# A fourth chunk of x turned by VectorE blocks in a hybrid attention and LRU layer

## The chip, the cores and the metric

The kernel runs on one core of one Trainium2 chip. Its time is the device time of one execution in microseconds; the table below gives the median of three runs of the kernel before. The profile is of one further execution. TensorE (PE in the profile) multiplies matrices, VectorE (DVE), ScalarE (ACT) and GpSimd (POOL) work elementwise, and SyncE (SP) issues most of the transfers between DRAM and the on-chip memory (SBUF).

## What is computed

One layer of an encoder for 512 tokens of width 2048, all in float32. Only the beginning matters here: an RMS norm and one projection, whose columns are then divided among attention heads, a linear recurrence and their gates.

```python
def hybrid_layer(x, norm_w, w_in, ...):
    h = rms_norm(x, norm_w)                       # x * rsqrt(mean(x*x) + eps) * norm_w
    proj = jnp.einsum('bsd,de->bse', h, w_in)     # (512, 2048) x (2048, 4608)
    q, k, v, g_attn, xr, g_lru = jnp.split(proj, SPLITS, axis=-1)
    attn_out = attention_group(q, k, v, q_norm_w, k_norm_w)
    lru_out = lru_group(xr, conv_w, conv_b, ...)
    mixed = jnp.concatenate([rms_norm(attn_out, attn_norm_w) * jax.nn.silu(g_attn),
                             rms_norm(lru_out, lru_norm_w) * jax.nn.silu(g_lru)], axis=-1)
    return x + jnp.einsum('bse,ed->bsd', mixed, w_out)
```

## The kernel before

Each float32 matrix is kept as two parts, a high one in the faster float32r format and a low one with what is left; a product is three matmuls (`mm3`: high by high, high by low, low by high). The rows of x enter the products without their norm: the factor per token, from the sum of the squares of its row, is multiplied in when the first sums are taken out of PSUM (`rbc`, line 471). So the squares are needed only when the first four sums are complete.

The first projection is `proj_feat(C_XR, a1, ...)`. It computes 512 columns of the recurrence's input in four PSUM banks and goes over the 2048 inner features in eight chunks (c = 0 to 7) of 256, two tiles of 128 each (kk = 2c and 2c + 1). A chunk needs the weights of its 256 features and x of these features *with the features along the partitions*. In DRAM x has the tokens along the rows, so it has to be turned. A chunk is 24 matmuls: four blocks of columns (e = 0 to 3) with six each, and after each block the generator yields the step (c, e).

`xchunk(c)` brings chunk c of x in several steps, taken one by one with `next`. Below, "x4" is the chunk c = 4 of x, "w4" the weights of chunk 4, and "s4" the splitting of these weights in high and low parts (`wsplit`, lines 218 and 219). There are two ways to turn:

- On TensorE (`xturn`), for c below `TURNED` = 5: load; eight transposes of 128 x 128 into PSUM (line 253); ScalarE takes the high part out with the norm's weight (258), VectorE the low part (261); VectorE squares the loaded chunk and sums along the row (272).
- By blocks, for c from 5 on: load; VectorE transposes blocks of 32 x 32 (`blocks`, 281), which leaves blocks in the wrong quarter of the partitions; `put_aside` writes them to DRAM with one transfer (289), `bring_back` reads them in the right order with four (296); ScalarE scales by the norm's weight (338) and casts the high part, VectorE subtracts for the low part (both 339). ScalarE squares the loaded chunk (268).

The order of instructions has three sources. TensorE's is that of the program. SP's is that of the program up to `s1.close()` (line 1234), and ScalarE's and VectorE's up to `s2.close()` (step (1, 2)). Everything else is placed by a planner, by readiness and by priority: `tc.high_priority(AHEAD)` raises the priority of what stands in its block by 600 places, and `tc.issue_after(i)`, or `behind(those)` for several, keeps what is in its block behind i on i's engine, without waiting for i's end. All engines execute their own queues in order; SP, too, waits with a transfer until its data and its buffer are there, and with it everything behind.

What happens at which step of the projection is written out in the table `moves` (line 1195): the entry (2, 0) "x5 x4 x5" takes one step of chunk 5, one of chunk 4 and one more of chunk 5 after the first block of chunk 2. A w loads weights, an s splits them. Loads of weights go through a ring with three places (`wring`), the split parts through four places each (`wh`, `wl`: two chunks).

The statistics (`xstats`, line 371) run in two steps, at (4, 3) and at (7, 0). The first adds up the eight chunks' squares on VectorE (373), takes the inverse root on GpSimd (346, 347) and lays the result out on VectorE (357 to 360). The second spreads it over the partitions with two matmuls on TensorE (367) and copies it (368). These two matmuls stand in TensorE's order behind step (7, 0).

Of the kernel before, what the change touches and what calls it, by code (L numbers as in the profile page):

```python
# [20 lines left out]
KT = DM // P  # L21
# [15 lines left out]
AHEAD = 600  # L37
# [12 lines left out]


B = 32
TURNED = 5
NQ = P // B


# [7 lines left out]
def hybrid_kernel(  # L64
# [20 lines left out]
    nc = tc.nc  # L85
# [32 lines left out]
    def nm(s):  # L118
        cnt[0] += 1
        return f"{s}_{cnt[0]}"  # L120

    def x2():
        return pools["xw"].tile([P, SEQ], F32R, tag="x2", bufs=32, name=nm("x2"))
# [19 lines left out]
    def mm():  # L143
        return ps.tile([P, SEQ], F32, tag="mm", name=nm("mm"))

    def const(shape, name, dt=F32):
        return cp.tile(list(shape), dt, tag=name, name=name)

    def f(ap):
        return ap.bitcast(F32)  # L150
# [58 lines left out]
    turn_of, split_done = [0], {}  # L209
# [19 lines left out]

    xh, xl = [None] * KT, [None] * KT  # L230
    ssq = const([P, NT, KT // 2], "ssq")
    highs, x_parts, squared = {}, [], []

    def xload(c, nk=1):

        xc = b4(shape=(P, NT, 2 * P))
        for k in range(nk):
            ks = slice(k * 2 * P // nk, (k + 1) * 2 * P // nk)
            cs = slice(c * 2 * P + ks.start, c * 2 * P + ks.stop)
            nc.sync.dma_start(xc[:, :, ks], xf[:, cs].rearrange("(t p) d -> p t d", p=P))  # L240
            yield xc

    def behind(those):
        stack = ExitStack()
        for ins in those:
            stack.enter_context(tc.issue_after(ins))
        return stack

    def xturn(xc, kk, then=None):
        pt = mm()  # L250
        for t in range(NT):
            ks = slice(kk % 2 * P, (kk % 2 + 1) * P)
            nc.tensor.transpose(pt[:, t * P : (t + 1) * P], xc[:, t, ks], ident)  # L253
        if then:
            then()
        xh[kk], xl[kk] = x2(), x2()
        with behind(split_done[-1] if kk > 3 else ()):
            highs[kk // 2] = nc.scalar.activation(
                xh[kk], pt, AF.Identity, scale=nw[:, kk : kk + 1]
            ).ins  # L260
        nc.vector.scalar_tensor_tensor(
            xl[kk], pt, nw[:, kk : kk + 1], f(xh[kk]), op0=ALU.mult, op1=ALU.subtract
        )

    def xsquare(xc, c):
        for t in range(NT):
            if c >= TURNED:
                nc.scalar.activation(
                    xc[:, t, :], xc[:, t, :], AF.Square, accum_out=ssq[:, t, c : c + 1]
                )  # L270
                continue
            square = nc.vector.scalar_tensor_tensor(
                xc[:, t, :], xc[:, t, :], 1.0, xc[:, t, :], op0=ALU.mult, op1=ALU.mult,
                accum_out=ssq[:, t, c : c + 1],
            )
            if c == 1:
                squared.append(square.ins)

    def blocks(u, t, src):

        nc.vector.transpose(
            u[:, :, :, t, :].rearrange("p b k r -> p k b r"),
            src.rearrange("p (k b c) -> p k b c", k=2, c=B),
        )

    def put_aside(u, tag, bufs):

        aside_ = dram.tile([P, NQ, 2 * SEQ // NQ], F32, name=nm(tag), tag=tag, bufs=bufs)
        nc.sync.dma_start(aside_, u.rearrange("p b k t r -> p b (k t r)"))
        return aside_  # L290

    def bring_back(to, aside_):

        src = aside_.rearrange("(i c) b x -> b c i x", c=B)
        for b in range(NQ):
            nc.sync.dma_start(
                to[b * B : (b + 1) * B].rearrange("p i k t r -> p i (k t r)"), src[b]
            )

    def in_order(v):  # L300
        return v.rearrange("p (t i r) -> p i t r", t=NT, i=NQ)

    def xchunk(c):
        with tc.high_priority(AHEAD):
            (xc,) = xload(c)
        yield
        if c < TURNED:
            with tc.high_priority(AHEAD):
                for k in range(2):
                    xturn(xc, 2 * c + k)  # L310
            if c == 2:
                yield
            with behind(split_done[2][1:] if c == 2 else ()):
                xsquare(xc, c)
            yield
            return
        u, back = (
            ring.tile([P, NQ, 2, NT, B], F32, name=nm("xu")) for ring in (aring, hring)
        )
        with tc.high_priority(AHEAD), tc.issue_after(squared[-1] if c == TURNED else split_done[3][1]):  # L320
            for t in range(NT):
                blocks(u, t, xc[:, t, :])
        yield
        with tc.high_priority(AHEAD):
            there = put_aside(u, "xd", KT // 2 - TURNED)
        with tc.issue_after(highs[TURNED - 1]):
            xsquare(xc, c)
        yield
        with tc.high_priority(AHEAD):
            bring_back(back, there)  # L330
        yield
        with tc.high_priority(AHEAD), behind(split_done[-1]):
            for k in range(2):
                kk = 2 * c + k
                xh[kk], xl[kk] = x2(), x2()
                hi, lo = (in_order(v) for v in (xh[kk], xl[kk]))
                v = back[:, :, k]
                nc.scalar.activation(v, v, AF.Identity, scale=nw[:, kk : kk + 1])
                x_parts[:] = nc.scalar.copy(hi, v).ins, nc.vector.tensor_sub(lo, v, f(hi)).ins
        yield  # L340

    last_pool = [None]
# [288 lines left out]
    def sent(es, nh, *us):  # L631

        us = us or [
            pools["rot"].tile([P, NQ, 2, NT, B], F32, tag="uq", bufs=2, name=nm("uq"))
            for _ in range(nh // 2)
        ]
        for n, u in enumerate(us):
            for t, e in enumerate(es):
                blocks(u, t, e[:, 2 * n : 2 * n + 2].rearrange("p h d -> p (h d)"))
            yield  # L640
            asides.append(put_aside(u, "qd", 5))
# [7 lines left out]
    def split_head(pair, k, hi, lo):  # L649
        src = pair[:, :, k]  # L650
        hi, lo = (in_order(v) for v in (hi, lo))
        return nc.scalar.copy(hi, src).ins, nc.vector.tensor_sub(lo, src, f(hi)).ins
# [509 lines left out]
    s2 = ExitStack()  # L1162
# [4 lines left out]
    with tc.high_priority():  # L1167
        xs, ws = xload(0, 2), wraw(w_in, 0, C_XR, 2)
        nc.scalar.dma_start(nw_st, norm_w.rearrange("(k p) -> k p", p=P))
        xc, raw = next(xs), next(ws)  # L1170
        next(xs), next(ws)
        table = const([P, 1], "table")
        nc.scalar.activation(table, ones[:, :1], AF.Exp)
        first = []

        def scales():
            columns(nw, nw_st)
            first.append(wsplit(raw, 0, nc.vector.tensor_copy))

        xturn(xc, 0, scales)  # L1180
        busy(WARM2)
    stats = xstats()
    chunks = [xchunk(c) for c in range(1, KT // 2)]

    raws = {}
# [5 lines left out]
    def split_x(c):  # L1191
# [1 line left out]
            given[c] = [wsplit(raws[c], k) for k in range(2)]  # L1193

    moves = {
# [6 lines left out]
    }  # L1202

# [8 lines left out]
    for step in proj_feat(C_XR, a1, first, given):  # L1212
        if step is None:
            with tc.high_priority():
                first.append(wsplit(raw, 1))
                xturn(xc, 1)
            xsquare(xc, 0)
            move(None)
            given[1] = wload(w_in, 2 * P, C_XR)
            continue  # L1220
        c, e = step
        move(step)
        if (c, e) == (1, 2):
            s2.close()
        if (c, e) == (4, 2):
            with tc.high_priority(AHEAD):
                vec_load()
        if (c, e) == (7, 1):
            columns(vec, vec_st)
        if (c, e) in ((4, 3), (KT // 2 - 1, 0)):  # L1230
            with tc.high_priority(AHEAD), tc.issue_after(split_done[-1][1]):
                next(stats)
# [216 lines left out]
```

## Time and profile before

| | |
|---|---|
| median of three runs | 627.94 us (627.38 to 628.29) |
| profiled execution | 627.43 us |
| its span, first to last instruction | 625.6 us |
| mean granted clock of TensorE | 0.999 |
| TensorE busy | 620.6 us, 99% of the span |
| VectorE, ScalarE, GpSimd busy | 79%, 56%, 16% |
| bytes moved by DMA | 127.61 MB, 204 GB/s on the mean |

A row of the timeline has the start and the duration in microseconds, the engine, the line, the operation, what it writes and reads, the shapes and how many instructions are merged into the row; in brackets stand the idle time of the engine ahead of it and what ended that. `SPq` is SP's queue: a row there is the issue of a transfer, not the transfer. Rows of groups give the busy time, the mean duration in nanoseconds of one instruction, and the idle time ahead. Names such as `b` (loaded x), `xu` (blocks of x, both before and after their way), `xd` (their copy in DRAM), `x` (high and low parts of x), `wr` (loaded weights) and `wh`, `wl` (their parts) are tiles.

### The profile page before, as it was taken

The numbers are of one execution on the slowest core, as the hardware profiler recorded it, in microseconds if no ns is written. First come the engines' busy times: TensorE is split into PE (matmuls) and PEld (weight loads), VectorE is DVE, ScalarE is ACT, GpSimd is POOL, SyncE is SP. The second block draws the span as 40 slices with busy tenths as digits, with TensorE's granted clock in tenths as the row PEclk, the third lists the DMA queues.
The fourth block names the chain that finished last, engine by engine and source line by source line (L and its number), as shares of the span: only waits on it lengthen the run. The fifth ranks groups of instructions, "written<-read, shape, count | busy, mean of one in ns | idle before, by whom it ended". The sixth has DMA issues, their size and how long they took to land.

```text
span 625.6 us, 8287 instructions
## 1 busy us (share of the span) xinstructions
PE 620.6 (99%) x2761; PEld 513.1 (82%) x2761; DVE 494.3 (79%) x795; ACT 353.1 (56%) x618; POOL 101.6 (16%) x134
## 2 busy tenths in 40 slices
PE   9999999999999999999999999999999999999997
PEld 7888888888888888888888888888888888888886
DVE  5967979986699876887887888549978866887886
ACT  3764899479946823545485548328445633443441
POOL 0000211112003621522123223100210101010010
PEclk9999999999999999999999999999999999999999
DMA  8987785759774599479669646923995777897262
GB/s 290 308 224 218 179 199 172 176 135 198 236 234 136 170 246 241 98 204 268 193 173 260 201 137 194 259 85 104 273 245 180 212 250 244 290 320 237 69 202 101
DMA packets 73595, 127.61 MB, mean 204 GB/s; under 512 B 6617, under 2 KB 29265, under 8 KB 73553
## 3 DMA queue, kind: packets, MB, share of 16 engines
q1 hardware_dynamic: 65664, 109.65, 56.5%
q0 software_dynamic: 7712, 17.31, 14.3%
q8 instruction: 21, 0.34, 0.2%
q14 instruction: 22, 0.17, 0.1%
q10 hardware_dynamic: 176, 0.14, 0.1%
HBM read 110.29 MB, written 37.75 MB: 237 GB/s over the span
## 4 chain that ended last, share of the span: by engine, by line
PE 99%; DVE 0%; issue 0%; POOL 0%; POOLq 0%
PE pj L153 21%; PE pj L155 21%; PE pj L154 21%; PE mm L1029 14%; PE pj L1029 11%; PE mm L155 3%; PE mm L153 3%; PE mm L154 3%; PE pj L388 1%; PE mm L253 1%; PE mm L1156 1%; PE mm L829 0%; PE mm L367 0%; DVE cb L1058 0%; PE mm L189 0%
## 5 line engine op out<-in xcount | busy, mean ns | idle before, releaser
L153 PE MATMUL pj<-x,wh 128*128 128x512 f32 x376 | 146.7, 390 | 0.0
L155 PE MATMUL pj<-x,wl 128*128 128x512 f32 x376 | 146.3, 389 | 0.0
L154 PE MATMUL pj<-x,wh 128*128 128x512 f32 x376 | 146.3, 389 | 0.0
L218 ACT CAST wh<-wr 128x512 fp32r<-128x512 f32 x143 | 85.1, 618 | 81.8 <-PE pj L154 32.0
L219 DVE TENSOR_TENSOR wl<-wr,wh 128x512 fp32r<-128x512 f32 x144 | 99.6, 720 | 21.3 <-ACT wh L218 20.2
L881 ACT CAST wh<-wr 128x1024 fp32r<-128x1024 f32 (+1 forms) x72 | 60.7, 860 | 74.8 <-PE mm L1029 35.4
L882 DVE TENSOR_TENSOR wl<-wr,wh 128x1024 fp32r<-128x1024 f32 (+1 forms) x72 | 68.7, 984 | 29.9 <-ACT wh L881 29.8
L155 PEld LDWEIGHTS pj<-x,wl 128*128 128x128 f32 x376 | 70.6, 188 | 14.8
L154 PEld LDWEIGHTS pj<-x,wh 128*128 128x128 f32 x376 | 70.6, 188 | 14.6
L153 PEld LDWEIGHTS pj<-x,wh 128*128 128x128 f32 x376 | 70.6, 188 | 14.5
L153 PE MATMUL pj<-wh,x 128*128 128x512 f32 x192 | 74.7, 389 | 0.0
L155 PE MATMUL pj<-wh,x 128*128 128x512 f32 x192 | 74.7, 389 | 0.0
L154 PE MATMUL pj<-wl,x 128*128 128x512 f32 x192 | 74.7, 389 | 0.0
L905 POOL DMA_DIRECT2D t<-in_w_out_dram x40 | 33.6, 897 | 157.1 <-DMA t<-in_w_out_dram 99.4
L1029 PE MATMUL mm<-wh,ml 128*128 128x512 f32 x126 | 49.0, 389 | 0.0
L1029 PE MATMUL mm<-wh,mh 128*128 128x512 f32 x126 | 49.0, 389 | 0.0
L1029 PE MATMUL mm<-wl,mh 128*128 128x512 f32 x126 | 49.0, 389 | 0.0
L154 PEld LDWEIGHTS pj<-wl,x 128*128 128x128 f32 x192 | 36.0, 188 | 7.6
L155 PEld LDWEIGHTS pj<-wh,x 128*128 128x128 f32 x192 | 36.0, 188 | 7.5
L153 PEld LDWEIGHTS pj<-wh,x 128*128 128x128 f32 x192 | 36.0, 188 | 7.4
L706 POOL TENSOR_SCALAR p<-p,sm 128x512 f32<-128x512 f32 x32 | 24.2, 762 | 88.7 <-DVE sm L705 88.7
L1029 PE MATMUL pj<-wl,mh 128*128 128x512 f32 (+1 forms) x100 | 38.5, 385 | 0.0
(201 smaller groups left out, 1041.0 us busy)
## 6 DMA issues: line engine op xcount, KB each, us to landing
wr<-in_w_in_dram SPq DMA_DIRECT2D x71, 512.0 KB, 4.8
wr<-in_w_out_dram SPq DMA_DIRECT2D x24, 512.0 KB, 5.1
t<-in_w_out_dram POOLq DMA_DIRECT2D x40, 256.0 KB, 7.0
wr<-t SPq DMA_DIRECT2D x40, 256.0 KB, 5.8
pd<-u SPq DMA_DIRECT2D x16, 512.0 KB, 3.0
pt<-pd SPq DMA_DIRECT2D x64, 128.0 KB, 4.0
t<-in_w_out_dram SPq DMA_DIRECT2D x24, 256.0 KB, 5.6
t<-t SPq DMA_DIRECT2D x16, 256.0 KB, 5.5
```

Source lines behind the costliest of these rows:

```text
L153: nc.tensor.matmul(acc, lh, rh, start=start, stop=False)
L154: nc.tensor.matmul(acc, lh, rl, start=False, stop=False)
L155: nc.tensor.matmul(acc, ll, rh, start=False, stop=stop)
L218: copy(hi, raw[:, k, :]).ins,
L219: nc.vector.tensor_sub(lo, raw[:, k, :], f(hi)).ins,
L253: nc.tensor.transpose(pt[:, t * P : (t + 1) * P], xc[:, t, ks], ident)
L388: nc.tensor.matmul(acc[e], w[:, e * P : (e + 1) * P], x_[k], start=k == 0 and j == 0, stop=False,)
L706: last_pool[0] = nc.gpsimd.tensor_scalar(p, p, sm, 0.0, op0=ALU.mult, op1=ALU.add).ins
L881: nc.scalar.copy(hi[:, to], b)
L882: nc.vector.tensor_sub(lo[:, to], b, f(hi[:, to]))
L905: nc.gpsimd.dma_start(dst, src, accum_op=ALU.add)
L1029: nc.tensor.matmul(dst[s][:, es], lh[:, ts_], rh[:, es], start=i == ends_[0] and j == 0, stop=i == ends_[1] and j == 2,)
```

## The change

`TURNED` becomes 4, so chunk 4 is turned by VectorE's blocks too: TensorE has eight transposes less. Its blocks do not go through DRAM. A new function, `carry`, moves them from SBUF to SBUF in twelve pieces of 32 partitions (32 KB each): nine issued by SP, three by GpSimd, and the four blocks that stay in their quarter are copied by GpSimd. Chunks 5 to 7 go through DRAM as before, `put_aside` and `bring_back` now with a step between them.

The squares of chunk 4 go from VectorE to ScalarE, behind the last high part that is taken out of PSUM. The squares of chunks 5 and 6 are put behind ScalarE's cast of chunk 5's high part, those of chunk 7 behind that of chunk 6. The block transposes of chunks 5 to 7 and the finishing of chunk 4 have new places to stand behind. The table of steps is written anew: the loads go out in the order x2 x4 w2 x3 x5 w3 x6 w4 x7 (before: x2 x3 w2 x5 x4 w3 x6 x7 w4), then the carry of x4, then x5's write, w5, x6's write, x5's way back, w6, x7's write, x6's and x7's way back, w7.

```diff
-TURNED = 5
+TURNED = 4
...
     def xsquare(xc, c):
...
-            square = nc.vector.scalar_tensor_tensor(
+            nc.vector.scalar_tensor_tensor(
...
+    def carry(to, u):
+
+        def at_(v, b):
+            return v[b * B : (b + 1) * B]
+
+        for d in range(1, NQ):
+            for b in range(NQ):
+                i = (b + d) % NQ
+                queue = nc.gpsimd if b == NQ - 1 else nc.sync
+                queue.dma_start(at_(to, b)[:, i], at_(u, i)[:, b])
+        for b in range(NQ):
+            nc.gpsimd.tensor_copy(at_(to, b)[:, b], at_(u, b)[:, b])
+
...
+    raw_x, blocked = {}, {}
+
+    def lows_of(c):
+        return {4: (), 5: (lows.get(2),), 6: split_done.get(3), 7: split_done.get(3)}[c][-1:]
 
     def xchunk(c):
...
-        with tc.high_priority(AHEAD), tc.issue_after(squared[-1] if c == TURNED else split_done[3][1]):
+        raw_x[c] = xc
+        with tc.high_priority(AHEAD), behind(lows_of(c)):
             for t in range(NT):
-                blocks(u, t, xc[:, t, :])
+                blocked[c] = blocks(u, t, xc[:, t, :])
         yield
         with tc.high_priority(AHEAD):
-            there = put_aside(u, "xd", KT // 2 - TURNED)
-        with tc.issue_after(highs[TURNED - 1]):
-            xsquare(xc, c)
-        yield
-        with tc.high_priority(AHEAD):
-            bring_back(back, there)
-        yield
-        with tc.high_priority(AHEAD), behind(split_done[-1]):
+            if c == TURNED:
+                carry(back, u)
+            else:
+                there = put_aside(u, "xd", KT // 2 - TURNED - 1)
+                yield
+                bring_back(back, there)
+        if c == TURNED:
+            with tc.issue_after(highs[c - 1]):
+                xsquare(xc, c)
+        yield
+        with tc.high_priority(AHEAD), behind(
+            (*split_done[-1], blocked[TURNED + 1]) if c == TURNED else split_done[-1]
+        ):
             for k in range(2):
...
                 nc.scalar.activation(v, v, AF.Identity, scale=nw[:, kk : kk + 1])
                 x_parts[:] = nc.scalar.copy(hi, v).ins, nc.vector.tensor_sub(lo, v, f(hi)).ins
+        for n in {5: (5, 6), 6: (7,)}.get(c, ()):
+            with behind(x_parts[:1]):
+                xsquare(raw_x[n], n)
         yield
...
     moves = {
-        None: "x1", (0, 2): "x1",
-        (1, 0): "x2", (1, 1): "x2", (1, 2): "x3 w2 s2 x2", (1, 3): "x3",
-        (2, 0): "x5 x4 x5", (2, 1): "x4 w3", (2, 2): "x6 x7", (2, 3): "w4 s3",
-        (3, 0): "x5 w5 x5 w6", (3, 1): "x6 x7 x6 x7", (3, 3): "s4 x5",
-        (4, 0): "x6 w7 x7", (4, 3): "s5 x6",
+        None: "x1", (0, 2): "x1 x2 x4",
+        (1, 0): "w2 x3 x4 x5", (1, 1): "x2", (1, 2): "w3 s2 x2", (1, 3): "x3",
+        (2, 0): "x6 w4 x7 x4", (2, 1): "x5", (2, 2): "x5 w5", (2, 3): "s3 x4",
+        (3, 0): "x6 x6 x5 w6", (3, 1): "x7 x7 x6", (3, 2): "x7", (3, 3): "s4 x5",
+        (4, 0): "w7", (4, 3): "s5 x6",
         (5, 3): "s6 x7", (6, 3): "s7",
     }
```

More of the change, by code (lines that the diff above doesn't have):

```diff
@@ L231, in hybrid_kernel @@
     ssq = const([P, NT, KT // 2], "ssq")
-    highs, x_parts, squared = {}, [], []
+    highs, lows, x_parts = {}, {}, []
     def xload(c, nk=1):
@@ L260, in xturn @@
             ).ins
-        nc.vector.scalar_tensor_tensor(
+        lows[kk // 2] = nc.vector.scalar_tensor_tensor(
             xl[kk], pt, nw[:, kk : kk + 1], f(xh[kk]), op0=ALU.mult, op1=ALU.subtract
-        )
+        ).ins
     def xsquare(xc, c):
@@ L275, in xsquare @@
             )
-            if c == 1:
-                squared.append(square.ins)
     def blocks(u, t, src):
-        nc.vector.transpose(
+        return nc.vector.transpose(
             u[:, :, :, t, :].rearrange("p b k r -> p k b r"),
             src.rearrange("p (k b c) -> p k b c", k=2, c=B),
-        )
+        ).ins
     def put_aside(u, tag, bufs):
```

## The prediction

> **What bounds the kernel now.** I read the page first (parts 1 and 4), then who waited for whom on TensorE, then TensorE's timeline around one group of transposes.
>
> ```profile
> span 625.6 us, 8287 instructions
> PE 620.6 (99%) x2761; PEld 513.1 (82%) x2761; DVE 494.3 (79%) x795; ACT 353.1 (56%) x618; POOL 101.6 (16%) x134
> PE 99%; DVE 0%; issue 0%; POOL 0%; POOLq 0%
> PE mm L1156 <- POOL ones L161: 1.1, 1, 1.1
> ```
>
> The lines are the span, the engines' busy time, the shares of the chain that ended last, and the one wait of TensorE. It is the whole chain, and its only wait is 1.1 us before its first instruction. So nothing can become faster except by taking instructions from TensorE, and anything can become slower that makes it wait. The change edits the first projection, up to about 50 us; behind it nothing is edited, and TensorE has no idle time there to win.
>
> **What is taken away.** One of the four groups of eight transposes of x (the fifth chunk, kk 8 and 9):
>
> ```profile
> 22.60 0.39 PE L154 MATMUL pj<-x,wh 128*128 128x512 f32 x1
> 22.83 0.39 PE L155 MATMUL pj<-x,wl 128*128 128x512 f32 x1
> 23.06 1.03 PE L253 MATMUL mm<-ident,b 128*128 128x128 f32 x8
> 23.85 0.48 PE L153 MATMUL pj<-x,wh 128*128 128x512 f32 x1
> 24.16 0.40 PE L154 MATMUL pj<-x,wh 128*128 128x512 f32 x1
> 24.40 0.39 PE L155 MATMUL pj<-x,wl 128*128 128x512 f32 x1
> ...
> 49.79 0.62 PE L367 MATMUL mm<-k,ones_r 128*128 128x512 f32 x2
> ```
>
> A row has start, duration, engine, line, operation and count. Durations overlap, so the starts count. Two matmuls are 0.23 us apart. From the last matmul before the group (22.83) to the third behind it (24.40) there are 1.57 us, where three steps of 0.227 would be 0.68: the group costs 0.89 us, of which 0.08 is the slower step behind it (23.85 to 24.16). From 23.85 to the sums of the statistics (49.79) there are 12 + 96 + 6 = 114 matmuls, 25.94 us or 0.227 each; a chunk of 24 takes 5.44. Chunks 4 to 7 then start, without the group, at 31.2, 36.7, 42.1 and 47.5, and L367 is due at 49.79 - 0.89 = 48.90.
>
> ```profile
> L253 PE MATMUL mm<-ident,b 128*128 128x128 f32 x40 | 5.8, 287 | 0.0
> ```
>
> The group's row gives 287 ns for one transpose, but 5.8 us busy for 40, so that they overlap. The Trainium skill (TensorE: Matmul & The Clock Gate, Part 4: PE-mode transpose) gives some 275 ns for one transpose in a kernel; taken as eight in a row that is an estimate of 2.2 us, and the kernel would gain that. The trace agrees with the figure as a duration, and not with the sum: eight starts lie within 0.79 us.
>
> **What is put in its place, one part at a time.** VectorE: two L261 (1.37 us by the row below) and four squares go; four block transposes (16.23 to 17.57, 1.34 us) and two subtractions (39.64 to 40.85, 1.21 us) come. ScalarE: two castings out of PSUM go; two scalings, two casts and four squares come, priced below. GpSimd: three transfers and four copies of 32 x 256.
>
> ```profile
> 16.23 1.42 DVE L281 STREAM_TRANSPOSE xu<-b 128x256 f32<-128x256 f32 x4 [1.21 <-DMA b<-in_x_dram]
> 17.57 1.37 DVE L261 SCALAR_TENSOR_TENSOR x<-mm,nw,x 128x512 fp32r<-128x512 f32 x2
> 39.64 1.29 DVE L339 TENSOR_TENSOR x<-xu,x 128x512 fp32r<-128x512 f32 x2 [1.97 <-ACT x L339]
> 40.85 0.69 DVE L219 TENSOR_TENSOR wl<-wr,wh 128x512 fp32r<-128x512 f32 x1
> L706 POOL TENSOR_SCALAR p<-p,sm 128x512 f32<-128x512 f32 x32 | 24.2, 762 | 88.7 <-DVE sm L705 88.7
> 34.74 0.20 POOL L346 TENSOR_SCALAR rstd<-xsum 128x4 f32<-128x4 f32 x1 [33.04 <-DVE xsum L373]
> ```
>
> VectorE has at most 1.34 + 1.21 - 1.37 = 1.2 us more, before the four squares come off. A GpSimd copy is bounded by 0.20 us (128 x 4) and 0.76 (128 x 512); I take 0.5, so 2 us for four, hidden in the 33.04 us in which GpSimd does nothing. If that cover failed, they would delay only x4. The block transposes of x4 find their data: it is the second load after w1 now, where x5 was the fourth and landed at 16.2 (the first row: VectorE waited for it). They stand where x5's stood and are done by 17.6, before the carry can start. x3 becomes that fourth load; its transposes are one group and twelve matmuls ahead of those at 23.06, at 23.06 - 0.89 - 12 x 0.227 = 19.45: nothing is lost by either.
>
> **The carried chunk (x4).** SP issues nine of its twelve transfers, behind all loads of x and w up to x7. Two limits of SP show before:
>
> ```profile
> 17.68 0.34 SPq L289 DMA_DIRECT2D xd<-xu  x1
> ...
> 24.65 1.76 SPq L296 DMA_DIRECT2D xu<-xd  x4
> ...
> 34.72 0.40 SPq L206 DMA_DIRECT2D wr<-in_w_in_dram  x1
> 35.21 1.84 SPq L296 DMA_DIRECT2D xu<-xd  x4
> 37.09 0.43 SPq L180 DMA_DIRECT2D vec_st<-in_conv_w_dram  x1
> 37.57 0.37 SPq L180 DMA_DIRECT2D vec_st<-in_conv_b_dram  x1
> 37.98 0.32 SPq L180 DMA_DIRECT2D vec_st<-in_lru_ba_dram  x1
> 39.22 0.31 SPq L180 DMA_DIRECT2D vec_st<-in_lru_bx_dram  x1
> ...
> SPq L296 <- DMA xd<-xu: 9.0, 2, 4.9
> SPq L180 <- DMA wr<-in_w_in_dram: 0.9, 1, 0.9
> DMA to landing us min/median/max: 2.6/3.0/4.9
> pd<-u SPq DMA_DIRECT2D x16, 512.0 KB, 3.0
> t<-in_w_out_dram POOLq DMA_DIRECT2D x40, 256.0 KB, 7.0
> ```
>
> First the rate: x5 landed at 16.2, and x5's write to DRAM, six transfers of 512 KB later, at 24.65 (it let SP go on): 1.40 us each. The loads ahead of the carry are the same number, so the last lands at 24.65 - 1.40, near 23.3. Second the depth: the load of lru_bx needs nothing of the core, yet waits for a load of w; it is the eighth transfer behind w7 (34.72). So SP keeps eight in flight. The eighth carry then waits for that last load at 23.3, the ninth for the first carry, which stands behind the same load. With 0.44 us an issue (1.76 for four) the ninth is issued near 23.8 and, by the least of the xu row (2.6), lands at 26.4; the row's longest (4.9) gives 28.7.
>
> ScalarE then scales, casts and splits w4. The prices:
>
> ```profile
> 28.62 0.40 ACT L268 ACTIVATE b<-b 128x256 f32<-128x256 f32 x1
> 29.02 0.40 ACT L268 ACTIVATE b<-b 128x256 f32<-128x256 f32 x1
> 29.42 1.32 ACT L338 ACTIVATE xu<-xu,nw 128x512 f32<-128x512 f32 x2
> 34.24 0.19 ACT L268 ACTIVATION_READ_ACCUMULATOR b<-b 128x1 f32 x1
> 37.76 1.34 ACT L338 ACTIVATE xu<-xu,nw 128x512 f32<-128x512 f32 x2 [3.33 <-DMA xu<-xd]
> 39.00 1.13 ACT L339 CAST x<-xu 128x512 fp32r<-128x512 f32 x2
> 40.03 1.14 ACT L218 CAST wh<-wr 128x512 fp32r<-128x512 f32 x2
> 34.46 0.19 DVE L373 TENSOR_REDUCE xsum<-ssq 128x4 f32<-128x32 f32 x1
> 36.39 1.29 DVE L360 TENSOR_TENSOR k<-ident,part 128x512 fp32r<-128x512 f32 x2
> ```
>
> From start to start a chunk's scalings and casts take 2.27 us (37.76 to 40.03) and a split of w 1.03 more (as the casts above it: two casts 39.00 to 40.03); a square 0.40. With x4 at 26.4 the last low half of w4 is there near 30.5; it is wanted five matmuls into chunk 4, at 32.3. So x4 may be 1.8 us late, up to 28.2, and costs nothing.
>
> **What is queued behind it.** x5's write to DRAM comes next on SP, near 24.3 instead of 17.68. A write of 512 KB by the pd row takes 3.0: landed at 27.3. Its way back before began at 24.65 and was used at 29.42, 4.8 later, behind one load; now w5 and x6's write are ahead. Least: 2.6 behind the fourth issue (1.3) is 3.9; most: 4.8 and one transfer more (1.4) is 6.2. So x5 is there between 31.2 and 33.5; I take 32.0, near the lower end because the queue has run empty. x5 is needed in chunk 5 at 36.7; ready with w5 about 36.5 for a low half wanted at 37.8: still no wait.
>
> **Where it comes due: the statistics.** Before, the twelve squares of x5 to x7 filled ScalarE's idle time and ended at 34.43 (34.24 + 0.19); the factors for L367 were ready at 37.68 (36.39 + 1.29), 3.25 later, 12 us ahead of TensorE. Now they stand behind x5's cast, without raised priority, while the finishing of x6 and x7 and the splits of w have it. From x5 on ScalarE has three chunks (3 x 2.27), three splits (3 x 1.03) and twelve squares (12 x 0.40): 14.7 us. If the squares come last, they end at 32.0 + 14.7 + 0.2 = 46.9, the factors are ready at 50.15, and L367 is due at 48.90: TensorE waits 1.25 us. That is the new end of a wait. The bounds of x5 give 0.45 to 2.75.
>
> **The sum.** -0.89 + 1.25 = +0.36 us: the forecast is no change that can be measured. On the profiled execution (627.43 us, 1.83 beyond its span) that is 627.79; on the median of the three runs (627.94), 628.3. What a measurement can tell from no change is about 0.2%, 1.26 us, so 626.7 to 629.2 is no change. The forecast's own range is 627.5 to 629.8.
>
> **Rivals.**
> - *The statistics are in time.* The order of ScalarE is planned, and gaps while x6 and x7 are on their way take squares; if x7's finishing or w7's split is put behind them, 1.0 to 3.3 us of the 14.7 fall away from this path and the wait vanishes. For it: the squares of before ran in just such gaps. Against: x5, x6 and x7 come closer together now. Time: 627.94 - 0.89 = 627.05.
> - *The statistics come much later.* x5 at its upper bound, and 0.8 us of gaps that no square fills: the wait is 3.5 us, the time 627.94 - 0.89 + 3.5 = 630.55. For it: DMA was full before (six transfers in a row at 1.40) and has the carry in addition. Against: the queue must run dry first, near 24.
> - *The other side by one mechanism: x4 itself is late.* A carry that takes the 7.0 us of a GpSimd transfer instead of 2.6 lands at 23.8 + 7.0 = 30.8, 2.6 behind the 28.2 from which it decides, and TensorE stands at the start of chunk 4: 627.94 - 0.89 + 2.6 = 629.65. For it: three pieces go by GpSimd, and the trace has no transfer from SBUF to SBUF. Against: GpSimd's pieces can start at 17.6 and have until 28.2, and even 7.0 us each fits.
> - *The transposes cost what their durations say.* 8 x 0.287 = 2.3 us: 625.65. Against: the starts above.
>
> **How the numbers follow.** The forecast 0.34, in time 0.28, much later 0.21, x4 late 0.14, full durations 0.03. Predicted: 628.3. No change holds most of the forecast (0.27) and of in time (0.20, its 627.05 lying 0.4 from the bound), and a little of x4 late (0.02): 0.49. Slower: 0.07 of the forecast, all of much later (0.21), 0.12 of x4 late: 0.40. Faster: 0.08 of in time and the full durations (0.03): 0.11. The range is 626.5 to 630.6: only the last rival and the worst of late arrivals lie outside.
>
> **What would show it.** TensorE has 32 instructions of L253, not 40, and the step between matmuls stays 0.227. Right: the chunks start at the times above, with a wait of TensorE at L367 for L360 of about a microsecond, and the last L268 of ScalarE near 47. A wait at L153 near 31 means that x4 was late; none anywhere, that the squares found gaps; x5's write issued by SP much before 24 would break the depth of eight. Wrong outright would be a wait behind 55 us, since nothing there is changed but its order.

## The result

| | before | after |
|---|---|---|
| median, same chip | 627.58 us (627.35 to 628.29, 6 runs) | 632.12 us (630.6 to 632.93, 6 runs) |
| profiled execution | 627.43 us | 631.33 us |
| its span | 625.6 us | 629.3 us |

The ratio is 1.0068, with a 95% interval from 1.0058 to 1.0079: the change made the kernel slower, by 4.5 us in the medians and 3.9 in the profiled executions, and 632.12 lies above the range of the prediction.

### The profile page after: what moved, and what is told of

It is laid out like the page before. It is cut to its first block, busy times and chain, and to the rows that moved or that the text cites. A ratio compares the mean times of both kernels' runs of the same rounds, so it can differ in the third digit from the quotient of the medians.

```text
span 629.3 us, 8311 instructions
## 1 busy us (share of the span) xinstructions
PE 621.8 (99%) x2753; PEld 511.9 (81%) x2753; DVE 495.1 (79%) x791; ACT 356.1 (57%) x628; POOL 107.7 (17%) x141
## 4 chain that ended last, share of the span: by engine, by line
PE 93%; DMA 3%; DVE 1%; SPq 1%; ACT 0%; issue 0%; POOL 0%; ACTq 0%; POOLq 0%
PE pj L155 19%; PE pj L154 19%; PE pj L153 19%; PE mm L1054 14%; PE pj L1054 11%; PE mm L154 3%; PE mm L155 3%; PE mm L153 3%; DMA b<-in_x_dram 2%; DMA xu<-xd 1%; PE mm L1181 1%; PE pj L413 1%; DMA xd<-xu 0%; DVE x L361 0%; DVE wl L219 0%; SPq L180 0%
## 5 line engine op out<-in xcount | busy, mean ns | idle before, releaser
L907 DVE TENSOR_TENSOR wl<-wr,wh 128x1024 fp32r<-128x1024 f32 (+1 forms) x72 | 68.7, 984 | 30.4 <-ACT wh L906 30.3
```

What stands on the lines that cost most here:

```text
L907: nc.vector.tensor_sub(lo[:, to], b, f(hi[:, to]))
```

## The profile after

The page's span and busy times, TensorE's row of transposes in the groups of instructions, and the view of who waited for whom on TensorE:

```profile
span 629.3 us, 8311 instructions
PE 621.8 (99%) x2753; PEld 511.9 (81%) x2753; DVE 495.1 (79%) x791; ACT 356.1 (57%) x628; POOL 107.7 (17%) x141
```

```profile
L253 PE MATMUL mm<-ident,b 128*128 128x128 f32 x32 | 4.8, 291 | 0.0
```

```profile
PE pj L153 <- ACT wh L218: 1.4, 2, 1.1
PE pj L155 <- DVE wl L219: 1.1, 4, 0.6
PE mm L1181 <- POOL ones L161: 1.1, 1, 1.1
```

TensorE has its eight transposes less. The wait ahead of its first instruction is the old one. The two other lines are new: TensorE now waits for the parts of the weights w. Where, its timeline shows (a row in which a wait ended has it in brackets; line 392 is the statistics' sum, line 367 before):

```profile
31.75 0.39 PE L154 MATMUL pj<-x,wh 128*128 128x512 f32 x1
32.37 0.50 PE L155 MATMUL pj<-x,wl 128*128 128x512 f32 x1 [0.23 <-DVE wl L219]
...
38.76 0.50 PE L153 MATMUL pj<-x,wh 128*128 128x512 f32 x1 [1.10 <-ACT wh L218]
...
39.65 0.50 PE L155 MATMUL pj<-x,wl 128*128 128x512 f32 x1 [0.16 <-DVE wl L219]
...
45.27 0.50 PE L153 MATMUL pj<-x,wh 128*128 128x512 f32 x1 [0.34 <-ACT wh L218]
...
46.16 0.50 PE L155 MATMUL pj<-x,wl 128*128 128x512 f32 x1 [0.16 <-DVE wl L219]
...
52.54 0.50 PE L155 MATMUL pj<-x,wl 128*128 128x512 f32 x1 [0.59 <-DVE wl L219]
...
53.58 0.63 PE L392 MATMUL mm<-k,ones_r 128*128 128x512 f32 x2
```

A wait costs more than its bracket, which counts from the end of the matmul before (31.75 + 0.39 = 32.14): the first is 0.23, but the starts are 0.62 apart instead of 0.227. Chunk 4 starts at 31.53. From there to line 392 are 78 matmuls, 17.7 us at the old step; they took 22.05. So 4.35 us are lost, all of them in chunks 4 to 7, and the 0.89 us of the transposes come off. Line 392 itself waits for nothing.

The next three views are SP's queue, ScalarE and VectorE in the same stretch.

```profile
16.65 8.97 SPq L307 DMA_DIRECT2D xu<-xu  x9
25.97 0.35 SPq L287 DMA_DIRECT2D xd<-xu  x1
26.42 0.38 SPq L206 DMA_DIRECT2D wr<-in_w_in_dram  x1
26.85 0.83 SPq L287 DMA_DIRECT2D xd<-xu  x1
28.97 1.94 SPq L294 DMA_DIRECT2D xu<-xd  x4
```

```profile
27.17 1.34 ACT L360 ACTIVATE xu<-xu,nw 128x512 f32<-128x512 f32 x2 [5.50 <-DMA xu<-xu]
...
35.82 1.34 ACT L360 ACTIVATE xu<-xu,nw 128x512 f32<-128x512 f32 x2 [3.63 <-DMA xu<-xd]
...
38.09 1.14 ACT L218 CAST wh<-wr 128x512 fp32r<-128x512 f32 x2
39.14 0.41 ACT L268 ACTIVATE b<-b 128x256 f32<-128x256 f32 x1
...
42.35 1.32 ACT L360 ACTIVATE xu<-xu,nw 128x512 f32<-128x512 f32 x2
...
47.25 1.32 ACT L360 ACTIVATE xu<-xu,nw 128x512 f32<-128x512 f32 x2
...
49.51 2.41 ACT L218 CAST wh<-wr 128x512 fp32r<-128x512 f32 x4
```

```profile
21.91 1.41 DVE L279 STREAM_TRANSPOSE xu<-b 128x256 f32<-128x256 f32 x4
23.25 1.36 DVE L261 SCALAR_TENSOR_TENSOR x<-mm,nw,x 128x512 fp32r<-128x512 f32 x2
24.53 1.41 DVE L279 STREAM_TRANSPOSE xu<-b 128x256 f32<-128x256 f32 x4
...
30.98 0.77 DVE L279 STREAM_TRANSPOSE xu<-b 128x256 f32<-128x256 f32 x2
31.67 1.25 DVE L219 TENSOR_TENSOR wl<-wr,wh 128x512 fp32r<-128x512 f32 x2
...
51.81 1.28 DVE L219 TENSOR_TENSOR wl<-wr,wh 128x512 fp32r<-128x512 f32 x2
```

SP issues the nine pieces of the carry until 25.6 and only then x5's write (25.97, before 17.68). Its way back goes out from 28.97, and ScalarE, after 3.63 us of idle time, begins x5 at 35.82 (before 29.42). From there it has no idle time until 50.5: x5, w5, eight squares from 39.14, x6 at 42.35, w6, four squares, x7 at 47.25, w7. TensorE, which wanted w5 at 37.5, has it 1.3 us late, and each later chunk is late again, because squares stand ahead of x6 and of x7. VectorE turned x6's blocks (21.91) before x5's (24.53), although x5 had been loaded by 17.2.

## Experiments

Four theories: **A**, x5's write is held, so x5 to x7 come late, and squares cost only where they stand ahead of a chunk that is due; **B**, the squares' new places are the cause; **C**, ScalarE and VectorE have too much work in any order; **D**, GpSimd's transfers land some 6 us after their issue, so that x4 is late. "x5 used" is the start of its scaling on ScalarE. "Lost" is TensorE's time from the start of its first matmul of chunk 4 to that of its last of chunk 7 beyond the 22.18 us of before (32.11 to 54.29 there, the statistics' sum in it), in the profiled execution. What TensorE loses right ahead of chunk 4 is not in it: 0.35 us in e4, 0.93 in e10 and 0.78 in e11. In before, e4, e6 and e10 ScalarE had no idle time ahead of x5's scaling, so that x5 may have been there earlier than "x5 used" says.

| run | median, us | ratio to before, 95% | x5's write | x5 used | lost |
|---|---|---|---|---|---|
| before | 627.5 to 627.8 | | 17.7 | 29.4 | 0 |
| after | 632.12 | 1.0058 to 1.0079 | 26.0 | 35.8 | 4.36 |
| e1 squares early | 629.84 | 1.0027 to 1.0052 | 26.2 | 36.3 | 2.56 |
| e2 no carry | 630.06 | 1.0028 to 1.0055 | 25.0 | 34.2 | 3.01 |
| e3 carry by GpSimd | 630.53 | 1.0033 to 1.0058 | 25.5 | 35.6 | 4.16 |
| e4 both, e1 and e3 | 630.15 | 1.0023 to 1.0048 | 21.2 | 35.2 | 1.81 |
| e5 carry 4/8, x5 first | 632.67 | 1.0064 to 1.0089 | 21.2 | 33.9 | 0 (5.05 at chunk 3) |
| e6 the same, squares moved | 629.64 | 1.0020 to 1.0043 | 21.5 | 35.6 | 2.19 |
| e7 before, squares late | 627.72 | 0.9989 to 1.0007 | 18.1 | 30.3 | 0.34 |
| e8 x5 first alone | 633.08 | 1.0072 to 1.0099 | 25.5 | 35.6 | 0 (5.95 at chunk 3) |
| e9 e5 with x3's high parts first | 628.33 | 1.0004 to 1.0022 | 21.2 | 32.2 | 1.06 |
| e10 e9, x4's squares together | 628.64 | 1.0009 to 1.0029 | 21.1 | 32.5 | 0.74 |
| e11 after, x4's squares together | 632.01 | 1.0058 to 1.0083 | 25.7 | 36.0 | 4.39 |
| e12 squares in idle stretches | 628.97 | 1.0018 to 1.0041 | 21.1 | 31.7 | 1.20 |
| e13 e12, statistics cut in two | 628.22 | 0.9999 to 1.0018 | 21.8 | 32.0 | 0.22 |
| e14 e13, carry 9/3 again | 631.07 | 1.0034 to 1.0060 | 25.8 | 35.7 | 3.18 |

### One part undone at a time (e1 to e4)

e1 puts the squares of chunks 5 to 7 back to where before had them; the rest is the change.

```diff
+        with tc.issue_after(highs[TURNED - 1]):
+            xsquare(xc, c)
...
-        for n in {5: (5, 6), 6: (7,)}.get(c, ()):
-            with behind(x_parts[:1]):
-                xsquare(raw_x[n], n)
```

> The changed kernel, with the squares of chunks 5 to 7 put back to where the kernel before has them (behind the last high part out of PSUM, nothing else to wait for). In the changed kernel's profile TensorE loses about 0.5 us at chunk 4, 1.8 at chunk 5, 1.05 at chunk 6 and 0.85 at chunk 7. Theory A (late arrival: x5 to x7 come too late because x5's write stands behind the carry on SP; the squares make it worse only where they stand ahead of x6 and w7): the losses at chunks 6 and 7 go (1 to 1.9 us), those at 4 and 5 stay: 630.2 to 631.1. Theory B (the squares' new places are the cause): all the losses go but that at chunk 4, 627.1 to 627.8. Theory C (ScalarE and VectorE have too much work, wherever it stands): 631.5 or more.

e2 leaves out the moving of chunk 4's blocks between the quarters of the partitions (its part of the product is therefore another); its price in time is what is wanted.

```diff
-                carry(back, u)
+                back = u
```

> The changed kernel without the carry: the blocks of chunk 4 are used where VectorE leaves them, so the moving of chunk 4's blocks between the quarters of the partitions (twelve transfers, four copies) is left out. Squares stay at their new places. Theory A: SP issues x5's write as soon as its blocks are there, near 23.3 instead of 26.0, x5 is used near 33 instead of 35.8, the losses at chunks 4 and 5 go (2.3 us) and part of those at 6 and 7: 628.5 to 629.9. Theory B: only chunk 4's loss goes, 631.0 to 631.6. Theory C: the copies and the transfers are not ScalarE's or VectorE's work, 631 or more.

e3 has all twelve pieces issued by GpSimd; e4 is e1 and e3 together.

```diff
-                queue = nc.gpsimd if b == NQ - 1 else nc.sync
-                queue.dma_start(at_(to, b)[:, i], at_(u, i)[:, b])
+                nc.gpsimd.dma_start(at_(to, b)[:, i], at_(u, i)[:, b])
```

> The changed kernel with all twelve pieces of the carry issued by GpSimd, none by SP; nothing is left out. By the profile a piece takes GpSimd 0.56 us to issue and a copy 0.71, so it is done issuing near 23.7 and copying near 26.5. Theory A: x5's write is issued near 23.3 as soon as its blocks are there, x5 is used near 33: 628.5 to 630, if x4 arrives by 28. Rival D (a transfer of GpSimd lands 6 us behind its issue, as its three did): x4 lands near 30, chunk 4 waits 2 to 3 us, 632 to 634. Theory B: 631.5 to 632.5.

> Both edits together: GpSimd issues the whole carry, and the squares of chunks 5 to 7 stand where the kernel before has them. Theory A with x4 in time: the losses at chunks 4 to 7 go nearly all, 626.7 to 628. Rival D: x4 late by 2 to 3 us and nothing else, 629 to 630.5. Theory B: as the first of these runs, 627.1 to 627.8. Theory C: 631 or more.

In e1 the gaps at chunks 6 and 7 are gone and those at 4 and 5 stay: the squares' places make 1.8 us of the loss (4.36 to 2.56), and neither A's nor B's interval held the time. e2 and e3 missed A's numbers for a reason that A had left out: with SP free of the carry, the write still went out only at 25.0 and 25.5, because VectorE turned x5's blocks behind x6's blocks and the low parts of x3. In e3 x5's are the first four of this row of VectorE, and the last four x7's:

```profile
24.09 2.72 DVE L279 STREAM_TRANSPOSE xu<-b 128x256 f32<-128x256 f32 x8
```

The write has two holders, each sufficient (that SP is one too, e8 below shows). e3's median is 1.6 under the changed kernel's; its profiled execution, the slowest of its five, does not show why. D falls with e3 as an account of the change: x4, with all its pieces on GpSimd, was used at 27.21, as in the changed kernel, and chunk 4 lost nothing. In e4, whose time lies in D's interval, x4 was used at 28.3 and was a little late; but most of its loss has another place. The planner happened to turn x5 first there, the write went out at 21.2, and yet x5 was used at 35.2: the early squares now stood directly ahead of it on ScalarE.

### Both holders of the write taken away (e5, e8), and the squares (e6, e7)

```diff
-                queue = nc.gpsimd if b == NQ - 1 else nc.sync
+                queue = nc.sync if d == 1 else nc.gpsimd
...
     def split_x(c):
-        with tc.high_priority(AHEAD), behind(x_parts):
+        with tc.high_priority(AHEAD), behind((*x_parts, *([blocked[5]] if c == 3 else ()))):
```

> The changed kernel with two edits: chunk 4's twelve pieces are carried four by SyncE and eight by GpSimd, and w3's low halves are issued behind x5's blocks, so that VectorE turns x5's blocks first. The squares stay where the change put them. A (x5's write is late behind the carry and behind other blocks on VectorE): the write is issued near 21 instead of 26, x5 is finished from near 33 instead of 35.8, the gaps at chunks 4 and 5 go (2.3 us), those at 6 and 7 stay in part, since the squares still stand ahead of x6's finishing: 628.0 to 629.3 us. B (the squares' places alone cost the time): only chunk 4's gap goes, 631.0 or more. C (ScalarE and VectorE have too much work in any order): 631.0 or more.

e8 is the second of these edits alone.

> The changed kernel with w3's low halves issued behind x5's blocks, so that VectorE turns x5's blocks first; the carry stays as it is. A with SyncE as the holder: x5's write still waits behind the carry's last piece near 25, it gains 0.5 us at most: 631.3 to 632.2 us. Rival (the order on VectorE is the holder): the write is issued near 22 to 23, x5 is finished near 33, 628.5 to 630.0 us.

In e8, one row of VectorE, one of SP's queue, three of TensorE and one stretch (length; busy time of PE, PEld, DVE, ACT and POOL; granted clock; DMA share; GB/s):

```profile
19.95 1.41 DVE L279 STREAM_TRANSPOSE xu<-b 128x256 f32<-128x256 f32 x4
```

```profile
25.55 0.53 SPq L287 DMA_DIRECT2D xd<-xu  x1
```

```profile
26.06 0.39 PE L155 MATMUL pj<-x,wl 128*128 128x512 f32 x1
28.96 0.80 PE L153 MATMUL pj<-x,wh 128*128 128x512 f32 x1 [2.51 <-ACT x L258]
...
30.34 0.63 PE L155 MATMUL pj<-x,wl 128*128 128x512 f32 x1
30.77 0.63 PE L153 MATMUL pj<-x,wh 128*128 128x512 f32 x1
```

```profile
28.00:32.00 4.00, 3.04 (x6) 2.11 (x7) 2.84 (x6) 4.00 (x12) 0.00 (x0) 0.56 0.95 300
```

x5's blocks are turned by 21.3, and its write waits until 25.55 behind the carry: SP alone holds it for 4 us. In e5 it goes out at 21.2. In both, chunks 4 to 7 lose nothing, but this shows nothing about the squares: TensorE came to chunk 5 only at 41.76 in e5 and 42.44 in e8, where it wanted w5 at 37.5 in the changed kernel, so that even the late x5 of e8 (35.6) was in time. Both times missed A's intervals (e5's lies where B and C had put it) by one new loss. In the planner's new order one of x3's two high parts (line 258) slid behind x4's finishing on ScalarE, and TensorE stood for it 2.51 us in e8 and 2.83 in e5; then its clock was lower for many matmuls.

e6 is e5 with the squares of x4 and x5 ahead of x4's finishing and those of x6 and x7 between w4's casts and x5's finishing:

```diff
+        if c == TURNED:
+            with tc.issue_after(highs[c - 1]):
+                xsquare(raw_x[5], 5)
+        if c == TURNED + 1:
+            with behind(split_done[-1][:1]):
+                xsquare(raw_x[6], 6)
+                xsquare(raw_x[7], 7)
...
-        for n in {5: (5, 6), 6: (7,)}.get(c, ()):
-            with behind(x_parts[:1]):
-                xsquare(raw_x[n], n)
```

> The kernel of the previous run with the squares in other places: x4's and x5's behind x3's high parts and ahead of x4's finishing, x6's and x7's between w4's casts and x5's finishing. A: with x5 early and no squares ahead of x6 and w7, no wait of TensorE stays at chunks 4 to 7, and what is left of the change is the 0.89 us of eight transposes: 626.7 to 627.4 us, under the kernel before. Rival (x5 and x6 arrive late for another reason, the transfers themselves): gaps of over 0.5 us stay at chunks 5 and 6, 628.0 us or more. C: 629 us or more.

```profile
35.19 0.40 ACT L268 ACTIVATE b<-b 128x256 f32<-128x256 f32 x1
...
35.59 1.32 ACT L369 ACTIVATE xu<-xu,nw 128x512 f32<-128x512 f32 x2
```

These rows are ScalarE's: the last square and its read-out run right up to x5's scaling, with no idle time between, so that x5 was not what ScalarE waited for. Nearly all of the 2.2 us were lost at chunk 5. The rival's time held, and its gap at chunk 5, but not the one at chunk 6, and not its reason. The squares cost wherever they stand ahead of a chunk that is due; this placing was my mistake.

e7 is the kernel before, TURNED = 5, with the squares put as in the change:

```diff
-        with tc.issue_after(highs[TURNED - 1]):
-            xsquare(xc, c)
+        raw_x[c] = xc
...
+        for n in {5: (5, 6), 6: (7,)}.get(c, ()):
+            with behind(x_parts[:1]):
+                xsquare(raw_x[n], n)
```

> The kernel before, with the squares of chunks 5 to 7 placed behind x5's and x6's casts as in the change; the fourth chunk is still turned by TensorE. A (the squares cost only where x5 is late): x5 is there at 29.4 and the squares end near 43, so that the statistics are ready before TensorE needs them: 627.4 to 628.3 us. B (the squares' new places are the cause by themselves): 629.0 us or more, with waits at chunks 6 and 7.

No difference from before, as A expected: the squares' new places cost nothing where x5 is used at 30.3. B falls as a cause by itself.

### The rest of the order mended (e9 to e12)

e9 is e5 with one more thing ahead of x4's finishing, e10 and e11 put x4's squares behind its second cast, in e9 and in the changed kernel.

```diff
-            (*split_done[-1], blocked[TURNED + 1]) if c == TURNED else split_done[-1]
+            (*split_done[-1], blocked[TURNED + 1], highs[c - 1]) if c == TURNED else split_done[-1]
```

```diff
-        if c == TURNED:
-            with tc.issue_after(highs[c - 1]):
-                xsquare(xc, c)
...
-        for n in {5: (5, 6), 6: (7,)}.get(c, ()):
+        for n in {4: (4,), 5: (5, 6), 6: (7,)}.get(c, ()):
```

> The kernel with the carry split four to eight and x5's blocks first (squares as in the change), with x4's finishing also held behind both of x3's high parts, which had slid behind it there and cost one gap of 3.2 us and a lowered clock after it. A (x5's late arrival is the cause, and the squares cost only what they push back): x5 is finished from near 33.9, the squares stand where ScalarE waits for x6 anyway, chunks 5 to 7 take 5.44 us each and chunk 4 at most 0.5 us more: 626.7 to 627.5 us, at or under the kernel before. Rival (the transfers themselves are late, or ScalarE's and VectorE's work is too much): chunks 5 to 7 still lose over 1 us in sum, 628.3 us or more.

> The previous kernel with x4's four squares behind x4's second cast instead of around its casts. A: chunk 4's own loss of about 0.5 us goes too, if it comes from the squares that stand between x4's casts: 626.3 to 627.1 us, under the kernel before. Rival (chunk 4 loses because x4's pieces land late): no difference from the previous kernel, within 0.2 us.

> The changed kernel with x4's four squares behind x4's second cast and nothing else changed. A: chunk 4's gap of 0.62 us goes, and the losses at chunks 5 to 7 stay, for x5's write and return are as before: 631.3 to 632.0 us. Rival (x4's pieces land late): chunk 4 keeps its gap and the time is that of the changed kernel, 632.0 to 632.6 us.

e9 loses nothing at chunks 4 and 5, 0.1 us at 6, and at chunk 7 this:

```profile
48.96 0.50 PE L155 MATMUL pj<-x,wl 128*128 128x512 f32 x1 [0.65 <-DVE wl L219]
```

Its median is 0.8 above A's interval and just at the lower end of the rival's. But the loss, down from 4.36 to 1.06 with all the work still there, is one wait for w7's low halves on VectorE, where the statistics stand ahead of them; e12 and e13 test that. In e10 and e11 chunk 4 lost more, not less: all four squares together went ahead of w4's casts. So that guess of mine on chunk 4 was wrong: e10's time lies in neither interval, and e11's (632.01) can't decide between its two.

e12 is e9 with ScalarE's squares of x4 and x5 in its idle stretch ahead of x4, VectorE's squares of x2 and x3 behind x4's subtractions, and those of x6 and x7 behind x5's casts.

```diff
-            (*split_done[-1], blocked[TURNED + 1], highs[c - 1]) if c == TURNED else split_done[-1]
+            (*split_done[-1], blocked[TURNED + 1], highs[c - 1], squares[4], squares[5])
+            if c == TURNED
+            else split_done[-1]
...
-        for n in {5: (5, 6), 6: (7,)}.get(c, ()):
-            with behind(x_parts[:1]):
+        for n in {4: (2, 3), 5: (6, 7)}.get(c, ()):
+            with behind(x_parts):
                 xsquare(raw_x[n], n)
```

> The kernel with the carry split four to eight, x5's blocks first and x3's high parts ahead of x4's finishing, and with the squares moved again: x4's and x5's, on ScalarE, ahead of x4's finishing, where that engine waited from 21 to 27; x2's and x3's, on VectorE, behind x4's subtractions; x6's and x7's behind x5's casts. A (the loss left at chunk 7, 1.0 us, comes from the statistics standing ahead of w7's low halves on VectorE, because x7's squares end only at 43.7): the statistics start near 40, the gap at chunk 7 goes, no wait of TensorE at chunks 4 to 7 is left, and the eight transposes' 0.89 us shows: 626.6 to 627.4 us against 627.6 before. Rival (the transfers of this kernel are too late wherever the squares stand): a gap of over 0.5 us stays at one of chunks 4 to 7, 627.9 us or more.

VectorE and TensorE of e12:

```profile
40.09 0.17 DVE L388 CAST part<-rstd 128x4 fp32r<-128x4 f32 x1 [1.55 <-POOL rstd L378]
...
42.79 1.28 DVE L219 TENSOR_TENSOR wl<-wr,wh 128x512 fp32r<-128x512 f32 x2
```

```profile
43.52 0.50 PE L155 MATMUL pj<-x,wl 128*128 128x512 f32 x1 [0.69 <-DVE wl L219]
```

A's time was missed, and the rival's gap of over 0.5 us is there. It left chunk 7, as A expected, and came back at chunk 6, for a reason that the trace names: the statistics now start early, and VectorE stands 1.55 us for GpSimd's inverse root, with w6's low halves behind it.

### The carry's split alone (e13 against e14)

e13 cuts the statistics: the sum and the root stay, the two diagonals come behind w6's low halves. e14 is e13 with the carry split nine to three as in the change; on every engine the two have the same order of work otherwise.

```diff
         rsqrt_mean(rstd, s, DM, NT)
+        yield
         yield from rows(rbc, rstd, lambda: k2(F32R, (P, NT, P)))
...
-        if (c, e) in ((4, 3), (KT // 2 - 1, 0)):
+        if (c, e) in ((4, 3), (5, 3), (KT // 2 - 1, 0)):
```

> The previous kernel with the statistics cut in two: the sum and the root stay behind w5's low halves, the two scaled diagonals for TensorE go behind w6's low halves on VectorE. A (what was left, 1.08 us at chunk 6, is VectorE standing still for GpSimd's root ahead of w6's low halves): no gap stays at chunks 4 to 7, 1.0 us under the previous kernel: 627.0 to 628.2 us, at best under the kernel before. Rival (the transfers' arrival scatters from one execution to the next, and that is what is left): 628.3 us or more, whatever the profiled execution shows.

> The same kernel with the carry put back to nine pieces on SyncE and three on GpSimd; every engine's order of work is the same, so that the two differ in the carry's split alone. A (nine pieces on SyncE hold x5's write): the write is issued near 25 instead of 21, x5 is finished from near 35 instead of 32, and TensorE loses some 1.5 us at chunk 5 and up to 1.0 more at chunk 6, where the squares then stand ahead of x6: 1.5 to 3.0 us over its sister. Rival (order on VectorE and ScalarE alone was the cause): within 0.5 us of its sister.

SP's queue, ScalarE and one stretch (columns as above) of e13:

```profile
21.77 0.35 SPq L287 DMA_DIRECT2D xd<-xu  x1
...
27.31 1.92 SPq L294 DMA_DIRECT2D xu<-xd  x4
```

```profile
32.01 1.34 ACT L366 ACTIVATE xu<-xu,nw 128x512 f32<-128x512 f32 x2 [1.42 <-DMA xu<-xd]
```

```profile
24.00:28.00 4.00, 4.00 (x20) 3.30 (x19) 3.25 (x8) 2.21 (x10) 0.00 (x0) 1.00 0.95 335
```

And of e14, with TensorE's two larger waits:

```profile
16.96 8.78 SPq L307 DMA_DIRECT2D xu<-xu  x9
25.84 0.53 SPq L287 DMA_DIRECT2D xd<-xu  x1
...
29.02 1.95 SPq L294 DMA_DIRECT2D xu<-xd  x4
```

```profile
35.70 1.34 ACT L366 ACTIVATE xu<-xu,nw 128x512 f32<-128x512 f32 x2 [5.00 <-DMA xu<-xd]
```

```profile
24.00:28.00 4.00, 4.00 (x19) 3.34 (x18) 3.15 (x8) 1.98 (x9) 0.00 (x0) 1.00 0.43 142
```

```profile
38.63 0.50 PE L153 MATMUL pj<-x,wh 128*128 128x512 f32 x1 [0.86 <-ACT wh L218]
...
45.15 0.50 PE L153 MATMUL pj<-x,wh 128*128 128x512 f32 x1 [0.31 <-ACT wh L218]
```

The nine pieces on SP cost 2.85 us by the medians, inside A's interval, and 2.96 by the loss. For VectorE's order there is no such pair; e2 and e3 show only that it holds the write when SP does not. While SP stands behind its own pieces, from 24 to 28, the core's DMA engines move 142 GB/s and are 43% busy; with four pieces on SP it is 335 and 95%. The transfers were not late for lack of DMA engines but because SP could not issue them. In e13's profiled execution TensorE has no wait in chunks 4 to 7, so C falls. Its median, 628.22 against 627.80, is 0.02 above A's interval and can't be told from the kernel before (0.9999 to 1.0018). So no version beat the kernel before, and one drew level.

## Why the prediction was wrong, by its own steps

**The transposes: right.** Chunk 2, which held the group, takes 5.54 us instead of 6.43: the 0.89 of the forecast. **The cover on GpSimd: right.** A copy takes 0.71 (four from 18.61 to 21.45), not 0.5, in time that nothing needs.

**The depth of eight on SP: right.** The nine issues of the carry stretch over 8.97 us, in which nine would need 4; SP's waits in them ended with the landing of loads of w (2.2 us) and x (1.4). The last load of x came 1.2 us later than the 23.3 of the forecast, and the last issue ended at 25.6 instead of 23.8.

**x4: nearly right.** Forecast 26.4, used at 27.17, still inside the 28.2 from which it was to decide; the rival "x4 is late" did not happen. But the forecast priced only the last low half of w4, wanted by the sixth matmul of chunk 4; the first is wanted by the third, at 31.98. VectorE began the two at 31.67 and had the last at 32.92 instead of 30.5. Right ahead of them it turned two of x7's blocks (30.98 in its view above). That is the 0.62 at 31.75. In e9, where no block stands there, x4 is used 0.3 earlier and chunk 4 loses nothing. What of the wait is due to those blocks and what to x4's squares stays open: e10 and e11 moved the squares and only made it larger.

**x5: this step failed.** The forecast was 24.3 + 3.0 + 4.7 = 32.0; the trace has 25.97 + 3.00 + 6.85 = 35.82. The write landed as priced. It was issued 1.7 later, for SP (25.6) and for VectorE (25.9), and the order on VectorE, where x5's blocks came third, had not been priced at all. The way back took 6.85, over the upper bound of 6.2: w5 and x6's write went out shortly ahead of it (26.42 and 26.85), and the DMA share was 0.92 from 28 to 32 and 1.07 from 32 to 36, against 0.69 from 24 to 28 in before. That this made it slow is likely, but no run takes it away. From the write's issue to x5's use the forecast had 7.7 us and 9.2 at most (3.0 + 6.2); in the eleven profiled executions in which ScalarE stood idle for x5 it was 9.3 (e2) to 12.7 (e5). The total of before, 11.7 us (17.68 to 29.42), would have given 24.3 + 11.7 = 36.0; that this meets the 35.82 is luck, since the write went out 1.7 later and took 1.9 less to x5's use. In e13 and e14 the total is 10.2 and 9.9, though the write alone took 5.5 and 3.2: what the write gains by going out into an empty queue, the way back loses.

**Where it came due: right in size, wrong in place.** The forecast gave ScalarE 14.7 us from x5 on; it took 14.7 (35.82 to 50.5), without idle time. With x5 at 35.82 its own formula gives factors at 35.82 + 14.7 + 0.2 + 3.25 = 53.97 for a sum due at 48.90, a wait of 5.07; the sum stands at 53.58, 4.68 late, of which 0.33 is a later start of chunk 4. So the mis-sized x5, with the squares behind it as the forecast had them, is enough for the size. But it came due not in one wait at the statistics: the planner put the squares not last but ahead of x6 and x7, and TensorE waited for w5, w6 and w7. The sentence "still no wait" for chunk 5 fell with x5, and the rival "much later" was the nearest, with 3.5 us of wait where 4.4 came.

**What was no cause.** Behind chunk 7 both profiled executions take the same (571.3 and 571.2 us), ahead of chunk 4 the changed one has won 0.58 of the 0.89 (31.53 against 32.11), and the share of the squares by themselves is nothing (e7). What stays open is why e9, e12 and e13 scatter more than before (e13 from 627.24 to 630.08): e9's profiled execution has 1.5 us more behind chunk 7 (e4's and e5's 1.4 and 1.8), where nothing was changed.

## What to carry to other kernels

Price a round trip through DRAM from issue to use by its own total in the trace of before, not by a median for its one half and a calm stretch for the other, and ask which holders the first transfer has: here SP's queue and VectorE's order each sufficed, and taking one away moved the write by 1.0 us at most. Small transfers on a queue that keeps only eight in flight block everything behind them for as long as the loads ahead take to land, while the DMA engines run half empty (43% busy in e14); give them to a queue with nothing behind it. And where an order is planned, one edit moves other work (a high part of x3, the casts of w4, the statistics): compare the order of all engines before a time is put down to the edit.

## What the runs showed of the hardware

The clock: in e8 TensorE stood 2.9 us from start to start (26.06 to 28.96), and the matmuls behind it were 0.43 us apart instead of 0.227, with a granted clock of 0.56 in that stretch; the wait of 1.10 us in the changed kernel did not do that. The Trainium skill (TensorE: Matmul & The Clock Gate, Part 1: The HAM clock gate) says that the clock goes to half after an idle window of about 3.4 us; the trace agrees with the half, but here a wait that shows as 2.51 us was enough. That made a short stall cost 5.95 us in chunk 3.

GpSimd's transfers, too, come eight deep. GpSimd's timeline in e3 and the group of its transfers (KB each, median us from issue to landing):

```profile
17.09 4.11 POOL L306 DMA_DIRECT2D xu<-xu  x8 [15.39 <-DVE xu L279]
23.29 0.50 POOL L306 DMA_DIRECT2D xu<-xu  x1 [2.08 <-DMA xu<-xu]
```

```profile
xu<-xu POOLq DMA_DIRECT2D x12, 32.0 KB, 5.4
```

The ninth of the twelve pieces waits for the landing of an earlier one. A piece of 32 KB from SBUF to SBUF took 5.4 us in the median, while the loads of x and w were still on their way.
